# The output gate's product moved behind the first attention step in a two-block model kernel

## The chip, the cores and the metric

One Trainium2 chip; the program uses one of its cores. The metric is the device time of one execution in microseconds (us).

## The reference, cut to what matters

Two model blocks run one after the other on one sequence of 256 tokens of width 1024. The change lies in the first mixer of the second block, which feeds one normalised input `h` to two branches and projects both back:

```
def mixer_ab(h, w_in, sinks, conv_w, a_log, dt_bias, norm_w, w_out, rel_bias):
    qa, ka, va, qkv_b, gate_b, beta_b, a_b = split_cols(h @ w_in, AB_SIZES)
    attn = swa_sink_attention(qa, ka, va, sinks, rel_bias)     # 8 query heads, 2 key heads, window 128
    qkv_b = silu(causal_dwconv(qkv_b, conv_w))
    ...
    o = gated_delta_rule(qb, kb, vb, g, beta)                  # 8 heads of 64, chunks of 64
    o = rmsnorm(o, norm_w) * silu(gate_b)
    return concatenate([attn, o]) @ w_out
```

Inside the delta rule each chunk needs the inverse of a unit lower triangular matrix (`Tm = triangular_solve(eye + L, eye)`), then products with it, and a short recurrence over the four chunks. The product that moves is `gate_b`: 1024 inputs to 512 columns, needed only when `o` is gated at the end.

## The kernel before

**Who orders the work.** The Python code gives instructions to a scheduler in program order. The scheduler writes one queue for each engine and one for the loads (SyncE's); of the instructions that are ready by its own model of time, the one given earlier goes first. A queue is then run strictly as written. `issue_after(x)` puts instructions behind `x` on its engine.

**Products.** Weights come as 1 MB blocks (512 rows, 512 columns) from DRAM into one of a few `raw` buffers (`fetch`, L393; three of them in this stage). `chunk` splits a block into a high and a low part: ScalarE casts the high part (L374), VectorE subtracts it for the low part (L339). The parts lie in four pairs of `hi`/`lo` buffers that all products share in turn. `mm3` does three matmuls for each pair of tiles (L354). `lin_a` puts tokens on the partitions: 2 token tiles x 8 row blocks x 3 = 48 matmuls of 128x512 for 512 columns. `lin_b` puts columns on the partitions: 96 matmuls of 128x256 for 512 columns. Their sums stand in four accumulators (`pd`).

**The stage.** `block2a` normalises, computes beta and decay, then the three products of the delta rule with their convolutions, and calls `delta`. `delta` prepares decay matrices and scores, sends a 16-block triangular matrix through DRAM (L1467, L1471), solves it on VectorE in 14 pairs of small products and differences (L1476 to L1480), and sends the result through DRAM again: two writes (L1481, L1483) and two reads (L1485). Then it calls `between()`, given by `block2a`: the gate's product, the queries, keys and values of the attention, and attention step 0. Behind it come the expansion of the solve's result into `U` and `T` by two 1024-wide products on VectorE, which stand behind step 0's last normalisation (`last_swa`, L1346), eight products that finish the inverse, and the recurrence with the gated output. Everything behind `between()` needs `U` and `T`.

**The attention.** `swa` runs four steps (two key heads, two halves of the sequence). One step: scores, softmax (a scaled add and a maximum on VectorE, four exponentials on ScalarE, four normalisations on VectorE, L1346), four or eight transposes (L357), a copy (L1353), the product with the values, a split. All steps share one pair of work buffers, so each waits for the one before. Step 0 is in `between()`, steps 1 to 3 are given behind `delta`.

**The end of the stage.** `out_part` multiplies with the output weights in two calls of 48 matmuls of 128x512: the first takes the attention's result, the second the delta rule's. The residual and the next normalisation follow.

```
self.delta(*qkv, g, sg, OH[1], OL[1], between)
with self.scope("d"):
    swa(order[1:])
ps = [[self.take("pd", 0) for _ in range(2)] for _ in range(2)]
self.out_part("ab_w_out_2", 0, ps, OH, OL, True, None)
```

Of the kernel before, what the change touches and what calls it, by code (L numbers as in the profile page):

```python
# [212 lines left out]
class K:  # L213
# [1411 lines left out]
    def block2a(self, x):  # L1625
        A, nc = self.A, self.nc
        W = A["ab_w_in_2"][0]
        ad = self.ada_a
        self.finish()
        H, L = self.split_units(8)  # L1630
        self.norm_mod(x, ad["a1"], ad["b1"], H, L, {-1: 10, 1: 8, 3: 6})
        st, mv = self.stat_of(H, L), self.mov_of(H, L)
        self.ada_b = self.ada2(1)
        OH, OL = self.split_units(8)
        with self.scope():
            self.cstt2 = self.unit()
            nc.sync.dma_start(self.cstt2[:, :NC2], A["cst2"])
            ba = self.tiny(32)
            self.rate = 0.0
            self.lin_few(W, 8, 2816, 16, mv, lambda t, p: nc.vector.tensor_copy(ba[:, t * 16 : t * 16 + 16], p))  # L1640
            g = self.delta_gates(ba)
            qkv = [self.take("u") for _ in range(3)]
            for cb in (1, 0, 2):
                u, y = qkv[cb], self.unit()

                def ev(ct, p):
                    yc = y[:, ct * 256 : ct * 256 + 256]
                    self.conv(yc, p, [self.vec("dn_conv_w_2", k * 12 + cb * 4 + ct, 1) for k in range(4)])
                    self.silu(yc)
                self.lin_b(W, 8, 768 + cb * 512, 512, mv, ev)  # L1650

                def post(u=u, y=y, cb=cb):
                    for t in range(2):
                        with self.scope():
                            p = self.psum()
                            for ct in range(4):
                                self.tr(p[:, ct * 128 : ct * 128 + 128], y[:, ct * 256 + t * 128 : ct * 256 + t * 128 + 128])
                            us = u[:, t * 512 : t * 512 + 512]
                            if cb == 2:
                                nc.scalar.copy(us, p)  # L1660
                            else:
                                v = lambda a: a.rearrange("p (h e) -> p h e", h=8)
                                self.act(us, p, AF.Square)
                                ss = self.tiny(8)
                                nc.vector.tensor_reduce(ss, v(us), axis=AX.X, op=ALU.add)
                                r = self.rsqrt(ss, 1.0, 8)
                                if cb == 0:
                                    self.ts(r, r, 0.125)
                                self.tt(v(us), v(p), r.unsqueeze(2).to_broadcast([128, 8, 64]), ALU.mult)
                    self.free(y)  # L1670
                self.posts.append(post)
            sg, aq, akv = self.unit(), self.unit(), self.take("ma")
            self.deepen(-1)
            bias, work = ([self.unit() for _ in range(2)] for _ in range(2))
            self.flush()
            perm = (lambda a: a.rearrange("p (g i d) -> p g i d", g=2, i=4), lambda a: a.rearrange("p (i g d) -> p g i d", g=2, i=4))

            self.rate = 0.0
            def between():
                self.lin_a(W, 8, 2304, 512, st, lambda t, p: self.silu2(sg[:, t * 512 : t * 512 + 512], p))  # L1680
                self.lin_b(W, 8, 0, 512, mv, lambda ct, p: nc.scalar.copy(aq[:, ct * 256 : ct * 256 + 256], p), perm)
                self.lin_b(W, 8, 512, 128, mv, lambda ct, p: nc.scalar.copy(akv[:, :256], p))
                self.lin_a(W, 8, 640, 128, st, lambda t, p: nc.scalar.copy(akv[:, 256 + t * 128 : 256 + t * 128 + 128], p))
                with self.scope("d"):
                    swa(order[:1])
            order = [(q4, qb) for q4 in range(2) for qb in range(2)]
            swa = lambda steps: self.swa(aq, akv[:, :256], akv[:, 256:], OH[0], OL[0], bias, work, steps)
            self.delta(*qkv, g, sg, OH[1], OL[1], between)
# [4 lines that stand above are left out]
            self.dbg("swa", OH[0].bitcast(F32))  # L1693
        self.free(*H, *L)
        self.rate = 1.55
        self.deepen(1)
        rate, self.rate = self.rate, 0.0
        with self.scope("d"):
            for k0 in (4,):
                self.out_part("ab_w_out_2", k0, ps, OH, OL, False, lambda t, cb, p: self.residual(x, ad["g1"], t, cb, p))  # L1700
            self.free(*ps[0], *ps[1])
        self.rate = rate
        self.free(*OH, *OL, ad["g1"])
        self.dbg("x3_0", x[0])

        H, L = self.split_units(8)
        self.norm_mod(x, ad["a2"], ad["b2"], H, L, {-1: 14, 3: 8})
        mv = self.mov_of(H, L)

        def up(cb, hh, hl):  # L1710
            n = 512 if cb < 5 else 256
            with self.scope():
                gt = self.unit()
                self.lin_b(A["ffn_w_gate_2"][0], 8, cb * 512, n, mv, lambda ct, p: self.act(gt[:, ct * 256 : ct * 256 + 256], p, AF.Silu))

                def ev(ct, p):
                    cs = slice(ct * 256, ct * 256 + 256)
                    m = self.med()[:, :256]
                    self.tt(m, p, gt[:, cs], ALU.mult)
                    self.split(m, hh[:, cs], hl[:, cs])  # L1720
                self.lin_b(A["ffn_w_up_2"][0], 8, cb * 512, n, mv, ev)
        self.deepen(4)
        self.deepen_split(1)
        self.ff_run([4] * 5 + [2], up, A["ffn_w_down_2"][0], x, ad["g2"])
        self.deepen(-4)
        self.deepen_split(-1)
        self.free(*H, *L, ad["g2"])
        self.dbg("x4_0", x[0])
        self.dbg("x4_1", x[1])
# [574 lines left out]
```

## Time and profile before

| | us |
|---|---|
| median of 3 runs | 2152.2 |
| lowest, highest | 2151.14, 2152.7 |
| the profiled execution | 2149.16 |
| its span, first to last instruction | 2147.3 |
| TensorE busy in the span | 2060.9 (96%) |
| VectorE busy | 1816.1 (85%) |
| ScalarE busy | 1305.4 (61%) |

The durations of instructions come from the profiled execution; a forecast made against it is carried over to the median. Matmuls are pipelined and their ends are modelled, so that a busy TensorE is not one at its peak. The stage of the change lies at about 640 to 812 us of the span.

### The profile page before, as it was taken

What the parts mean: (1) busy time and instruction counts of PE and PEld (TensorE: products, weight loads), DVE (VectorE), ACT (ScalarE), POOL (GpSimd) and SP (SyncE); (2) the same over time, 40 slices, a digit from 0 to 9 for tenths busy, and PEclk for the clock granted to TensorE, in tenths of its full rate; (3) what the DMA queues carried; (4) which work ended last, traced back from release to release, by engine and by line L of the source; (5) the groups of instructions that cost most, each with busy time, mean ns of one, the idle gap of its engine ahead of it and who ended that gap; (6) DMA issues with size and microseconds to landing.
All of it is one profiled execution on the core that took longest, in us unless ns stands there. A gap on an engine that the chain in (4) does not pass through costs nothing. (4 is left out here: it accounts for less than half of the span.)

```text
span 2147.3 us, 31020 instructions
## 1 busy us (share of the span) xinstructions
PE 2060.9 (96%) x11593; PEld 1700.0 (79%) x11593; DVE 1816.1 (85%) x2645; ACT 1305.4 (61%) x1833; POOL 2.1 (0%) x6
## 2 busy tenths in 40 slices
PE   6999999999999999999999999999999999999987
PEld 5987887889988879998997887677767876677764
DVE  6888985898888868888787988998888898897887
ACT  4544354454445435444765887877777687777676
POOL 0000000000000000000000000000000000000000
PEclk9999999999999999999999999999999999999998
DMA  7545767878843527885465999999999999999994
GB/s 307 194 165 213 264 220 254 299 294 299 303 164 119 151 101 272 309 337 207 144 259 188 351 346 380 371 362 338 368 358 395 341 353 368 376 369 338 363 362 174
DMA packets 99996, 610.70 MB, mean 284 GB/s; under 512 B 19155, under 2 KB 24060, under 8 KB 27772
## 3 DMA queue, kind: packets, MB, share of 16 engines
q1 hardware_dynamic: 99836, 608.64, 75.8%
q8 instruction: 92, 1.51, 0.3%
q14 instruction: 68, 0.56, 0.1%
HBM read 606.75 MB, written 3.42 MB: 284 GB/s over the span
## 5 line engine op out<-in xcount | busy, mean ns | idle before, releaser
L354 PE MATMUL pd<-k 128*128 128x512 f32 (+2 forms) x7144 | 1390.8, 349 | 39.9 <-DVE k L339 30.9
L339 DVE TENSOR_TENSOR k<-k,k 128x1024 fp32r<-128x1024 f32 (+2 forms) x1125 | 1205.3, 1112 | 205.7 <-ACT k L374 201.2
L354 PEld LDWEIGHTS pd<-k 128*128 128x128 f32 (+1 forms) x7144 | 1087.7, 188 | 266.1 <-DVE k L339 82.3
L374 ACT CAST k<-k 128x1024 fp32r<-128x1024 f32 (+2 forms) x1107 | 1019.1, 974 | 374.9 <-PE pd L354 187.7
L354 PE MATMUL ps<-k 128*128 128x512 f32 (+7 forms) x3295 | 637.9, 345 | 13.8 <-DVE k L339 3.7
L354 PEld LDWEIGHTS ps<-k 128*128 128x128 f32 (+4 forms) x3295 | 476.3, 178 | 116.6 <-DVE k L339 15.1
L348 DVE SCALAR_TENSOR_TENSOR k<-k,k 128x512 f32<-128x512 f32 (+1 forms) x257 | 188.5, 735 | 2.1 <-ACT k L351 0.2
L351 ACT ACTIVATE k<-k 128x256 f32<-128x256 f32 (+8 forms) x142 | 69.0, 500 | 79.4 <-DVE k L339 41.6
L351 ACT ACTIVATE k<-pd 128x256 f32<-128x256 f32 (+1 forms) x120 | 55.4, 486 | 95.2 <-PE pd L354 92.5
L339 DVE TENSOR_TENSOR k<-k 128x512 f32<-128x512 f32 (+13 forms) x277 | 93.8, 356 | 16.9 <-ACT k L351 12.1
L354 PEld LDWEIGHTS ps<-k,k 128*128 128x128 f32 x606 | 92.0, 197 | 16.1 <-DVE k L348 2.9
L354 PE MATMUL ps<-k,k 128*128 128x64 f32 (+4 forms) x606 | 87.8, 266 | 3.2 <-DVE k L348 2.7
L357 PE MATMUL ps<-k,k 128*128 128x128 f32 (+1 forms) x416 | 64.2, 279 | 16.4 <-DVE k L343 15.5
L339 DVE TENSOR_TENSOR k<-ps,k 128x512 fp32r<-128x512 f32 (+5 forms) x111 | 63.5, 579 | 16.6 <-PE ps L354 7.4
L357 PEld LDWEIGHTS ps<-k,k 128*128 128x128 f32 (+1 forms) x416 | 51.0, 144 | 30.7 <-DVE k L343 18.2
L339 DVE TENSOR_TENSOR k<-pd,k 128x512 f32<-128x512 f32 (+3 forms) x96 | 53.0, 569 | 13.7 <-PE pd L354 9.5
L351 ACT ACTIVATE k<-ps,k 128x128 f32<-128x128 f32 (+2 forms) x104 | 38.9, 448 | 41.8 <-DVE k L348 26.7
L2140 ACT COPY k<-pd 128x512 f32<-128x512 f32 x28 | 16.4, 587 | 56.4 <-PE pd L354 56.3
L348 DVE SCALAR_TENSOR_TENSOR k<-pd,k,k 128x255 f32<-128x255 f32 (+2 forms) x96 | 43.1, 475 | 4.4 <-ACT k L351 4.0
L345 DVE TENSOR_SCALAR k<-ps,k 128x128 f32<-128x128 f32 (+1 forms) x94 | 34.0, 405 | 10.0 <-PE ps L354 6.9
L348 DVE SCALAR_TENSOR_TENSOR k<-k 128x256 f32<-128x256 f32 (+7 forms) x121 | 37.0, 312 | 3.0 <-ACT k L351 1.3
L348 DVE SCALAR_TENSOR_TENSOR k<-ps,k 128x512 f32<-128x512 f32 (+1 forms) x34 | 23.6, 715 | 11.4 <-PE ps L354 11.0
(92 smaller groups left out, 376.9 us busy)
## 6 DMA issues: line engine op xcount, KB each, us to landing
k<-in_moe_w_up_dram SPq DMA_DIRECT2D x112, 1024.0 KB, 7.2
k<-in_moe_w_gate_dram SPq DMA_DIRECT2D x112, 1024.0 KB, 7.4
k<-in_moe_w_down_dram SPq DMA_DIRECT2D x112, 1024.0 KB, 7.4
k<-in_ada_w_dram SPq DMA_DIRECT2D x48, 1024.0 KB, 6.0
k<-in_w_in_dram SPq DMA_DIRECT2D x44, 1024.0 KB, 5.7
k<-in_w_ff_dram SPq DMA_DIRECT2D x32, 1024.0 KB, 6.2
k<-in_w_ada_dram SPq DMA_DIRECT2D x24, 1024.0 KB, 6.9
k<-in_cd_w_in_dram SPq DMA_DIRECT2D x14, 1024.0 KB, 4.9
```

Source lines behind the costliest of these rows:

```text
L339: return self.nc.vector.tensor_tensor(o, a, b, op=op)
L345: self.nc.vector.tensor_scalar(o, a, s1, s2, op0=op0, op1=op1)
L348: self.nc.vector.scalar_tensor_tensor(o, a, s, b, op0=op0, op1=op1)
L351: return self.nc.scalar.activation(o, a, f, **kw)
L354: return self.nc.tensor.matmul(o, l, r, start=start, stop=stop, skip_group_check=skip)
L357: return self.nc.tensor.transpose(o, i, self.ident[: i.shape[0], : i.shape[0]])
L374: self.last_hi = self.nc.scalar.copy(hi, src)
L2140: nc.scalar.copy(gu, pu)
```

## The change

The gate's `lin_a` (columns 2304 to 2815) is given to the scheduler as the last part of `between()` instead of the first: behind the attention's queries, keys, values and step 0, and still ahead of `U` and `T`, of attention steps 1 to 3 and of the output projection. No instruction is added or taken away.

```
             def between():
-                self.lin_a(W, 8, 2304, 512, st, lambda t, p: self.silu2(sg[:, t * 512 : t * 512 + 512], p))
                 self.lin_b(W, 8, 0, 512, mv, lambda ct, p: nc.scalar.copy(aq[:, ct * 256 : ct * 256 + 256], p), perm)
                 self.lin_b(W, 8, 512, 128, mv, lambda ct, p: nc.scalar.copy(akv[:, :256], p))
                 self.lin_a(W, 8, 640, 128, st, lambda t, p: nc.scalar.copy(akv[:, 256 + t * 128 : 256 + t * 128 + 128], p))
                 with self.scope("d"):
                     swa(order[:1])
+                self.lin_a(W, 8, 2304, 512, st, lambda t, p: self.silu2(sg[:, t * 512 : t * 512 + 512], p))
```

## Rows read from the trace of the kernel before

**Rows 1.** The page, busy time of each engine over the whole span.
```profile
PE 2060.9 (96%) x11593; PEld 1700.0 (79%) x11593; DVE 1816.1 (85%) x2645; ACT 1305.4 (61%) x1833; POOL 2.1 (0%) x6
```
**Rows 2.** Busy time by stretch: length, busy us, instructions; granted clock, DMA share, GB/s.
```profile
684.00:692.00 8.00, 4.86 (x18) 3.17 (x17) 8.00 (x37) 2.74 (x7) 0.00 (x0) 0.82 0.14 30
...
708.80:732.40 23.60, 23.33 (x187) 22.55 (x185) 21.88 (x56) 11.00 (x22) 0.00 (x0) 1.00 0.71 229
732.40:741.50 9.10, 5.26 (x28) 3.83 (x28) 6.75 (x15) 3.36 (x11) 0.00 (x0) 0.75 0.71 169
741.50:784.70 43.20, 41.85 (x644) 33.67 (x642) 27.86 (x73) 11.88 (x37) 0.00 (x0) 0.97 0.11 38
784.70:793.60 8.90, 5.72 (x36) 4.19 (x35) 6.35 (x29) 4.04 (x13) 0.00 (x0) 0.62 0.62 216
```
**Rows 3.** VectorE in order of time, 728 to 742 us: start, length, instructions.
```profile
728.39 3.00 DVE L339 TENSOR_TENSOR k<-k 128x56 f32<-128x56 f32 x13
732.17 0.69 DVE L348 SCALAR_TENSOR_TENSOR k<-pd,k 128x512 f32<-128x512 f32 x1 [0.78 <-PE pd L354]
...
734.50 0.68 DVE L1336 TENSOR_REDUCE k<-k 128x4 f32<-128x512 f32 x1
...
735.69 0.35 DVE L339 TENSOR_TENSOR k<-k,k 128x4 f32<-128x4 f32 x2
736.07 0.17 DVE L343 TENSOR_SCALAR k<-k 128x4 f32<-128x4 f32 x1
737.96 0.16 DVE L339 TENSOR_TENSOR k<-k 128x4 f32<-128x4 f32 x1 [1.71 <-ACT k L351]
738.15 0.18 DVE L1344 RECIPROCAL k<-k 128x4 f32<-128x4 f32 x1
738.37 0.87 DVE L1346 TENSOR_SCALAR k<-k 128x128 f32<-128x128 f32 x4
739.16 2.35 DVE L339 TENSOR_TENSOR k<-k 128x1024 f32<-128x1024 f32 x2
```
**Rows 4.** The same view of SyncE's queue of loads, from 717 us.
```profile
717.30 10.27 SPq L393 DMA_DIRECT2D k<-in_ab_w_out_dram  x4
731.41 0.33 SPq L1481 DMA_DIRECT2D scr<-k  x1
```
**Rows 5.** The instructions of L1485, the reads back from DRAM: first and last start, landing.
```profile
L1485 SPq DMA_DIRECT2D k<-scr x2: 370/750/1131, 733.5 to 734.1; - x2
...
DMA to landing us min/median/max: 2.8/3.2/3.7
```
**Rows 6.** TensorE's group of 128x512 matmuls, 741.5 to 793.58, then to 813 us: xcount, busy, mean ns.
```profile
L354 PE MATMUL pd<-k 128*128 128x512 f32 x16 | 5.4, 446 | 0.0
...
L354 PE MATMUL pd<-k 128*128 128x512 f32 x80 | 18.4, 390 | 0.0
```
**Rows 7.** All engines in order of time, near 788 and 794 us.
```profile
787.92 1.97 PE L357 MATMUL pd<-k,k 128*128 128x128 f32 x8 [3.18 <-DVE k L1346]
...
794.15 0.69 DVE L339 TENSOR_TENSOR k<-ps,k 128x512 fp32r<-128x512 f32 x1 [0.28 <-ACT k L374]
```
**Rows 8.** TensorE's groups: 681 to 708.8, then 708.8 to 732.4 us.
```profile
L354 PE MATMUL pd<-k 128*128 128x512 f32 x36 | 11.6, 452 | 1.4 <-DVE k L339 1.4
...
L354 PE MATMUL pd<-k 128*128 128x256 f32 x116 | 14.1, 283 | 0.0
```
**Rows 9.** VectorE's groups, 684 to 715.5 us.
```profile
L339 DVE TENSOR_TENSOR k<-k,k 128x512 fp32r<-128x512 f32 x8 | 5.0, 684 | 0.0
...
L348 DVE SCALAR_TENSOR_TENSOR k<-k,pd 128x512 f32<-128x512 f32 x2 | 1.4, 688 | 0.5 <-ACT k L351 0.5
```
**Rows 10.** VectorE's groups during the solve, 715.5 to 731.3 us.
```profile
L339 DVE TENSOR_TENSOR k<-k 128x512 f32<-128x512 f32 x8 | 5.5, 684 | 0.0
L339 DVE TENSOR_TENSOR k<-k,k 128x1024 fp32r<-128x1024 f32 x4 | 4.9, 1217 | 0.0
L339 DVE TENSOR_TENSOR k<-k,k 128x512 fp32r<-128x512 f32 x3 | 2.1, 687 | 0.0
```

More of the change, by code (lines that the diff above doesn't have):

```diff
@@ L1679, in between @@
             def between():
-                self.lin_a(W, 8, 2304, 512, st, lambda t, p: self.silu2(sg[:, t * 512 : t * 512 + 512], p))
                 self.lin_b(W, 8, 0, 512, mv, lambda ct, p: nc.scalar.copy(aq[:, ct * 256 : ct * 256 + 256], p), perm)
@@ L1685, in between @@
                     swa(order[:1])
+                self.lin_a(W, 8, 2304, 512, st, lambda t, p: self.silu2(sg[:, t * 512 : t * 512 + 512], p))
             order = [(q4, qb) for q4 in range(2) for qb in range(2)]
```

## The prediction

> **What bounds the kernel now.** I read the page first, for the whole span: TensorE is busy 96% of it and VectorE 85% [rows 1]. The change touches one stage of about 130 us, so I cut that stage with the view of busy time by stretch, at the places where TensorE's queue changes character [rows 2]. The reader should see three kinds of stretch. From 684 to 692 us VectorE is full (8.00 of 8.00) and TensorE starves. From 708.8 to 732.4 TensorE is full (23.33 of 23.60) and VectorE nearly so (21.88). From 732.4 to 741.5 nobody is full: TensorE works 5.26 of 9.10 us, VectorE 6.75, and the granted clock averages 0.75. A second such hole lies at 784.7 to 793.6 us (5.72 of 8.90, clock 0.62). A move of work inside a stage can gain only what it puts into those two holes.
>
> Next, what makes the first hole. VectorE's order of time [rows 3] shows the triangular solve ending with 13 short operations without a break (728.39, 3.00 us), then the softmax of attention step 0 (732.17 to 739.2), with a wait of 1.71 us on ScalarE inside it, and at 739.16 the two products that expand U and T (2.35 us), which the whole delta chain waits for. They stand behind step 0's last normalisation by an explicit order. Their other input comes through DRAM: SyncE's queue sends the result off from 731.41 us [rows 4] and issues the two reads at 733.5 and 734.1; they land 2.8 to 3.7 us later [rows 5], so by 737.8 us at the latest. So at 739.16 it is step 0's softmax, and not the transfer, that ends last, by 739.16 - 737.8 = 1.4 us.
>
> Last, what makes the second hole and the end of the stage. TensorE's groups by stretch [rows 6] show that of the 96 matmuls 128x512 of the output projection (two calls of 48) 16 run before 793.58 us and 80 after. The second 48 need the delta rule's result, whose split only starts at 794.15 [rows 7]; the other 32 of the first 48 wait for attention step 3, whose transposes start at 787.92 after TensorE waited 3.18 us for its normalisation [rows 7].
>
> **What is removed and added.** Nothing; 48 matmuls, four splits, two tanh, two products and two 1 MB loads get a lower rank. Their costs:
>
> TensorE: 48 matmuls 128x512. 80 of them took 18.4 us, 0.23 us each [rows 6], so 11.0 us. Now 36 of the 48 run before 708.8 us [rows 8] and the last 12 behind that.
>
> VectorE: four low-part splits of 1.217 us [rows 10], 4.9 us, and the two silu products of 0.688 us [rows 9], 1.4 us. ScalarE pays as many casts and two tanh, and is idle more than half of 684 to 732.4 us [rows 2], so I cost it at nothing; if that cover went, the splits would be late, which is the first rival.
>
> Cover taken away from the starved stretch 684 to 692: costed at nothing, because the queries' splits step into the place. One of them is 0.684 us of VectorE for 12 matmuls of 14.1/116 = 0.122 us [rows 8, 9], that is 2.1 us of TensorE work for a us of VectorE; the gate's is 1.217 us for 12 of 0.23 us, 2.3 us. And VectorE, not TensorE, is the bound there [rows 2]. Without any cover TensorE's idle 3.1 us could grow by its 4.86 busy us.
>
> SyncE's queue: the two gate loads go behind the five of queries, keys and values, and come to stand ahead of the four of the output weights (717.30 and on) and in the neighbourhood of the DRAM writes of 731.41 [rows 4]. An issue takes 0.33 us, nothing beside the 4 us without an issue between 727.57 and 731.41; what one costs that has to wait for its buffer belongs to the first rival.
>
> **What the order becomes.** Without 11.0 us of gate ahead of them, queries (96 matmuls), keys (24) and values (48) are through TensorE earlier, between 4 us (only the 12 late gate matmuls and their waits are saved) and 11 us (all of it); I take 8, since the splits still have to share VectorE. Then step 0's softmax, which starts at 732.17 now [rows 3], can start near 724 and fits into the solve as filler, and the gate's 11.0 us of matmuls lie, with step 0's own, between 724 and 738 us, across the first hole.
>
> Does the solve end later for it? VectorE ran out of filler at 728.4 us [rows 3]: in the solve it carried 8 products of 0.684 us, four 1024-wide splits (one of the values, three of the output weights) and three 512-wide ones beside its own pairs [rows 10]. Afterwards the gate's four splits take the place of the output weights' three, which must wait until the gate's matmuls give up their shared split buffers. The count up to the end of the solve changes by minus 3 x 1.217 (output weights, 3.7), minus 1.4 (silu, later now), plus step 0's softmax: 0.69 + 0.68 + 0.35 + 0.17 + 0.16 + 0.18 + 0.87 = 3.1 us [rows 3]. All three: -2.0. Bounds: -5.1 (the first two alone) and +3.1 (the last alone). I take 0, which is within a us of the middle between them, since a split that goes can be replaced by whatever else is ready.
>
> **First term.** The solve ends where it did, the transfer lands by 737.8, step 0 is done before: U and T start 1.4 us earlier. With the bounds: from 1.7 us lost (1.4 - 3.1) to 6.5 gained (1.4 + 5.1).
>
> **Second term.** Attention steps 1 to 3 follow one another through one pair of work buffers. With step 0 out of the way some 8 us earlier, less what the gate takes of the hole, step 3 no longer comes last, and matmuls of the first projection call fill the second hole. At least nothing (step 3 is held back by the delta chain, which ranks higher); at most 32 x 0.23 = 7.4 us, all that is left over from the first call. I take the idle time that TensorE shows there before step 3's transposes, 3.2 us [rows 7]: it is nearest to a row.
>
> How much room TensorE has ahead of that hole is read in two ways. Between 741.5 and 784.7 us matmuls cover 41.85 of 43.20 us, which would leave no room; weight loads cover 33.67 [rows 2]. [...] No row here settles which reading holds; that is the third rival.
>
> **Sum.** 1.4 + 3.2 = 4.6 us, 0.21%. The profiled execution took 2149.16 us (span 2147.3), 3.0 us less than the median of the runs, 2152.2; it would become 2144.6, and the median 2147.6. What measurement of this kernel tells from no change is about 0.2%, 4.3 us, so the forecast lies just beyond that edge.
>
> **Rivals.**
> 1. Slower: the gate spills into the delta chain. It now ranks above U and T and everything behind them, and its splits wait for buffers, for loads and for one accumulator that step 0's scores hold. If its matmuls run after 739 us, they stand in TensorE's queue between the small dependent matmuls of the chain. Price: 11.0 us less the idle of the first hole, 9.10 - 5.26 = 3.8 [rows 2]: 7.2 us later, minus the 1.4: 5.8, so 2158.0. It decides if fewer than half of the gate's matmuls are done when U and T start. For it: four splits more have to fit a VectorE that is 21.88 of 23.60 full. Against it: the buffers come free with the queries, 8 us earlier than now. Chance 0.15. [...]
> 2. Same: the gain is given back. The output weights' three splits (3.7 us) now fall into 741.5 to 784.7 us. VectorE is free 15.3 of 43.2 us there [rows 2], but each can hold a link of the chain by up to 1.2 us; with two held, the first term is gone, and with step 3 held back by the chain, the second. 2152 within 2 us. Chance 0.25.
> 3. More: all 32 left-over matmuls get out of the tail, 7.4 + 1.4 = 8.8, so 2143.4. [...] Against it: step 3's rank. Chance 0.12.
>
> **How the numbers follow.** The forecast has the remaining 0.48, with its own range from 2145 (a little of rival 3) to 2150 (half of it): 0.28 of that is beyond 4.3 us, 0.20 not. Faster: 0.28 + 0.12 = 0.40. Slower: 0.15 and 0.02 of rival 2, 0.17. Same: 0.20 + 0.23 = 0.43. The range holds the forecast, rival 2 and the greater part of rivals 1 and 3: 2143 to 2157.5.
>
> **What the profile would show.** Right: step 0's softmax on VectorE before the solve's end, U and T starting at or before 738 us with the transfer as the last releaser, 128x512 matmuls in what was the first hole, and fewer than 80 after the final split. Wrong: U and T later than 739, gate matmuls between the chain's after it, or the step order reached but still 80 in the tail. What would make it wrong above all is a solve that ends later because step 0's softmax sits inside it.

## The result, and the profile after

The changed kernel took 2165.09 us in the median of 8 runs (2157.66 to 2166.07), the kernel before 2152.28 (2151.14 to 2153.09): ratio 1.0053, 95% interval 1.0043 to 1.0062. It is 12.8 us slower; the forecast was 2147.6, its range 2143 to 2157.5. The runs of this kernel, and of all that give the queries first, spread more than those of before, and the long ones have the lower mean granted clock (2157.66 us at 0.991, 2166.07 at 0.986). The profiled execution took 2165.35 us, 16.2 more than the 2149.16 of the one before.

Busy time by stretch (columns as in [rows 2]); first the kernel before from 692 us on, then the changed kernel:

```profile
692.00:700.00 8.00, 7.96 (x65) 7.05 (x65) 5.87 (x19) 4.78 (x10) 0.00 (x0) 0.96 0.26 105
700.00:708.00 8.00, 8.00 (x141) 6.54 (x140) 7.59 (x14) 2.99 (x5) 0.00 (x0) 1.00 0.29 68
708.00:716.00 8.00, 8.00 (x56) 7.35 (x55) 7.54 (x13) 4.01 (x8) 0.00 (x0) 1.00 0.50 93
```

```profile
684.00:692.00 8.00, 2.34 (x10) 1.31 (x9) 8.00 (x37) 2.96 (x8) 0.00 (x0) 0.65 0.01 3
692.00:700.00 8.00, 8.00 (x42) 7.55 (x40) 4.88 (x17) 2.31 (x5) 0.00 (x0) 0.50 0.01 3
700.00:708.00 8.00, 8.00 (x68) 6.94 (x69) 3.17 (x6) 2.15 (x4) 0.00 (x0) 0.50 0.08 16
708.00:716.00 8.00, 6.62 (x91) 5.64 (x87) 5.67 (x11) 1.84 (x3) 0.00 (x0) 0.50 0.09 19
716.00:724.00 8.00, 8.00 (x52) 8.00 (x51) 5.74 (x10) 1.83 (x3) 0.00 (x0) 0.72 0.47 111
```

The reader should read the last but two column, the granted clock. In the starved stretch TensorE worked 2.34 us instead of 4.86 [rows 2], and then ran at 0.50 for the 24 us in which the delta rule's decay matrices, transposes and scores are made. It shows as busy for 22.6 us of them, but finishes 42 + 68 + 91 matmuls where before there were 65 + 141 + 56, with the gate's wide ones among them. VectorE, busy for 21.0 of those 24 us before, is now idle for 10.3 of them. In the kernel before, TensorE had these wide matmuls right behind the starved stretch:

```profile
691.32 2.45 PE L354 MATMUL pd<-k 128*128 128x512 f32 x7
```

The start of the solve on VectorE in the kernel before, then VectorE of the changed kernel in order of time, which answers to [rows 3, 9, 10]:

```profile
715.50 1.12 DVE L339 TENSOR_TENSOR k<-k 128x256 f32<-128x256 f32 x3
```

```profile
690.74 0.68 DVE L339 TENSOR_TENSOR k<-k,k 128x512 fp32r<-128x512 f32 x1
...
715.00 3.69 DVE L339 TENSOR_TENSOR k<-k,k 128x512 fp32r<-128x512 f32 x6
...
728.29 0.42 DVE L339 TENSOR_TENSOR k<-k 128x256 f32<-128x256 f32 x1 [1.14 <-DMA k<-scr]
...
734.41 5.68 DVE L339 TENSOR_TENSOR k<-k 128x36 f32<-128x36 f32 x24
740.01 0.68 DVE L348 SCALAR_TENSOR_TENSOR k<-pd,k 128x512 f32<-128x512 f32 x1
...
746.45 0.87 DVE L1346 TENSOR_SCALAR k<-k 128x128 f32<-128x128 f32 x4
747.24 2.35 DVE L339 TENSOR_TENSOR k<-k 128x1024 f32<-128x1024 f32 x2
```

Of the queries' eight splits one ran at 681.26, one at 690.74, and the other six only at 715.00, behind the last score product. The solve starts at 728.29 instead of 715.50 and ends at 740.1 instead of 731.4; step 0's softmax still comes behind it (740.01), and U and T start 8.1 us later than in [rows 3], 1.0 of which is that the whole stage began later in this execution. SyncE's queue, in the kernel before and then, against [rows 4], in the changed one:

```profile
710.46 0.39 SPq L1471 DMA_DIRECT2D k<-scr  x1
```

```profile
717.55 5.03 SPq L393 DMA_DIRECT2D k<-in_ab_w_in_dram  x2
722.76 0.38 SPq L1471 DMA_DIRECT2D k<-scr  x1
...
740.12 0.33 SPq L1481 DMA_DIRECT2D scr<-k  x1
```

The read of the solve's input (L1471) now stands behind two loads, the second of which is held up until 722 us; the data came at 728.29, 5.5 us behind the issue. TensorE in order of time, against [rows 7, 8]; first the start of the delta chain in the kernel before:

```profile
741.55 5.09 PE L354 MATMUL ps<-k 64*64 64x64 f32 x128
```

```profile
691.47 1.65 PE L354 MATMUL pd<-k 128*128 128x256 f32 x6 [1.69 <-DVE k L339]
...
715.91 21.16 PE L354 MATMUL pd<-k 128*128 128x256 f32 x160
740.98 7.37 PE L354 MATMUL pd<-k 128*128 128x512 f32 x24 [3.91 <-ACT k L1682]
...
748.77 6.30 PE L354 MATMUL pd<-k 128*128 128x512 f32 x31
755.00 4.38 PE L354 MATMUL ps<-k 64*64 64x64 f32 x128
```

The split of 690.74 released 6 matmuls, not 12. The gate's 128x512 matmuls lie on both sides of U and T (747.24), 24 in the first group and 23 in the second (with 8 of step 0's product), and the chain's first product starts at 755.00, 7.8 us behind U and T instead of 2.4. The gate began late because it takes over the accumulator of the values' second half, whose copy (L1682) stood on ScalarE behind the copy of the solve's result:

```profile
740.13 0.63 ACT L1482 COPY k<-k 128x256 f32<-128x256 f32 x1 [6.52 <-DVE k L339]
740.66 0.27 ACT L1682 COPY k<-pd 128x128 f32<-128x128 f32 x1
```

Last the tail. Here are VectorE's rescaling in the next normalisation (L343), the mark of the stage's end used below, in the kernel before and then in the changed one, and the changed kernel's 128x512 matmuls behind the final split (805.71 us):

```profile
814.93 0.75 DVE L343 TENSOR_SCALAR k<-k 128x1024 f32<-128x1024 f32 x1
```

```profile
831.22 0.75 DVE L343 TENSOR_SCALAR k<-k 128x1024 f32<-128x1024 f32 x1
```

```profile
L354 PE MATMUL pd<-k 128*128 128x512 f32 x84 | 19.7, 395 | 0.0
```

84 instead of 80 [rows 6]: nothing got out of the tail, and step 3's last matmuls are now in it. From final split to mark it lasts 25.5 us instead of 20.8. The account of the 16.3 us between the marks: U and T 8.1 later, the way from them to the chain 5.4 longer, the chain to the final split 1.9 shorter (50.7 us instead of 52.6), the tail 4.7 longer.

### The profile page after: what moved, and what is told of

Read it like the earlier page. It is cut to its first block, busy times and chain, and to the rows that moved or that the text cites. A ratio compares the mean times of both kernels' runs of the same rounds, so it can differ in the third digit from the quotient of the medians.

```text
span 2163.6 us, 31016 instructions
## 1 busy us (share of the span) xinstructions
PE 2072.6 (96%) x11593; PEld 1710.0 (79%) x11593; DVE 1818.2 (84%) x2645; ACT 1305.9 (60%) x1833; POOL 2.1 (0%) x6
## 5 line engine op out<-in xcount | busy, mean ns | idle before, releaser
L354 PE MATMUL pd<-k 128*128 128x512 f32 (+3 forms) x7144 | 1393.0, 349 | 42.0 <-DVE k L339 30.3
L354 PEld LDWEIGHTS pd<-k 128*128 128x128 f32 (+1 forms) x7144 | 1091.2, 189 | 268.8 <-DVE k L339 84.3
L354 PE MATMUL ps<-k 128*128 128x512 f32 (+7 forms) x3295 | 645.2, 349 | 13.0 <-DVE k L339 4.1
L354 PEld LDWEIGHTS ps<-k 128*128 128x128 f32 (+4 forms) x3295 | 482.9, 182 | 116.9 <-DVE k L339 15.0
L351 ACT ACTIVATE k<-k 128x256 f32<-128x256 f32 (+8 forms) x142 | 69.1, 499 | 75.5 <-DVE k L339 37.0
L339 DVE TENSOR_TENSOR k<-k 128x512 f32<-128x512 f32 (+11 forms) x277 | 94.8, 356 | 21.2 <-ACT k L351 13.2
L348 DVE SCALAR_TENSOR_TENSOR k<-ps,k 128x512 f32<-128x512 f32 (+1 forms) x34 | 23.5, 713 | 11.4 <-PE ps L354 11.0
```

What stands on the lines that cost most here:

```text
L339: return self.nc.vector.tensor_tensor(o, a, b, op=op)
L348: self.nc.vector.scalar_tensor_tensor(o, a, s, b, op0=op0, op1=op1)
L351: return self.nc.scalar.activation(o, a, f, **kw)
L354: return self.nc.tensor.matmul(o, l, r, start=start, stop=stop, skip_group_check=skip)
```

## The experiments

The table gives medians, the ratio to the kernel before with its interval, and from each profiled execution three times counted from VectorE's first sum of squares for the normalisation of the delta rule's inputs (L1665, at 670.4 to 673.7 us; called the stage's start below): the read of the solve's input, U and T, and the mark; between the last two, the way from U and T to the chain's first product.

| kernel | median us | ratio (95%) | read | U and T | to chain | mark |
|---|---|---|---|---|---|---|
| before | 2152.28 | 1 | 39.8 | 68.5 | 2.4 | 144.2 |
| changed | 2165.09 | 1.0053 (1.0043 to 1.0062) | 51.1 | 75.5 | 7.8 | 159.5 |
| e1 cover | 2160.46 | 1.0038 (1.0025 to 1.0052) | 44.8 | 69.8 | 7.9 | 153.8 |
| e2 accumulators | 2164.81 | 1.0050 (1.0033 to 1.0067) | 51.2 | 75.7 | 8.6 | 160.4 |
| e3 gate before step 0 | 2165.16 | 1.0063 (1.0045 to 1.0081) | 43.1 | 75.7 | 2.4 | 152.5 |
| e4 gate behind queries | 2163.31 | 1.0049 (1.0036 to 1.0063) | 46.6 | 81.8 | 2.4 | 158.5 |
| e5 row blocks outermost | 2161.49 | 1.0042 (1.0027 to 1.0057) | 42.7 | 67.4 | 8.0 | 150.4 |
| e12 the same, one run | 2164.42 | | 49.0 | 74.2 | 9.0 | 159.4 |
| e6 read first | 2162.95 | 1.0046 (1.0032 to 1.0060) | 46.6 | 73.5 | 9.0 | 158.6 |
| e7 gate behind the inverse | 2170.79 | 1.0092 (1.0078 to 1.0105) | 50.2 | 74.7 | 4.6 | 170.9 |
| e8 four edits | 2156.90 | 1.0022 (1.0013 to 1.0031) | 38.0 | 63.5 | 9.1 | 147.6 |
| e9 U and T free, gate first | 2155.72 | 1.0018 (1.0009 to 1.0027) | 41.1 | 67.6 | 2.4 | 147.7 |
| e10 constant matmuls | 2156.57 | 1.0022 (1.0013 to 1.0030) | 42.5 | 68.3 | 6.5 | 152.0 |
| e13 half of the change | 2149.84 | 0.9985 (0.9976 to 0.9994) | 40.1 | 67.4 | 1.9 | 144.6 |
| e14 a quarter | 2157.80 | 1.0023 (1.0013 to 1.0033) | 39.4 | 68.4 | 5.1 | 151.1 |
| e15 three quarters | 2158.60 | 1.0022 (1.0012 to 1.0033) | 44.8 | 68.7 | 5.7 | 151.2 |

The profiled execution of e3 was its shortest run (2158.09 us), that of e5 one of its shorter ones (2157.48); those of e1 and e10 (2163.63, 2160.08) lie above the median, and those of e2 and e6 (2166.36, 2166.01) were their longest.

**e1, cover for the starved stretch.** Constant matmuls first in `between()`:

```
             def between():
+                with self.scope("d"):
+                    self.warm(30)
+                self.q["pd"].rotate(1)
```

> The changed kernel (median 2165.1 us) with 30 matmuls of 128x512 on constants, whose sums nobody reads, given first in between(): a filler for TensorE that needs no split. Clock theory (TensorE starves at 684 to 692 us, its clock falls to half until 721, and so the scores and the solve come late): the clock stays at full speed from 684 to 721 us, U and T start near 741 instead of 747.2 us, and the time falls by 5 to 8 us, to 2157 to 2160, although 30 x 0.23 = 6.9 us of matmuls were added. Rival (the new order of the queues delays the scores, the clock only accompanies it): U and T stay at 746 to 748 us and the time at 2164 us or above.

4.6 us came back, though 30 matmuls were added, a little less than expected. The clock held at 1.00 from 684 to 700 us, then fell to 0.58 and 0.57 (700 to 708 and 708 to 716), where only the small products were left.

**e10, the shadow of the gate.** 24 constant matmuls of 128x512 on the way to the solve, where the gate's had stood:

```
+        self.warm(12)
         chan_tr(kn, kT)
...
             score(kT, Lr, q)
+            self.warm(6)
```

> The changed kernel with 24 constant matmuls of 128x512 where the gate's stood in the kernel before: 12 ahead of the keys' transposes in the delta rule, 6 behind each of the two score products. They compute nothing that is used, stand on the path to the solve and cost TensorE some 5.5 us at the full clock. Clock theory (what delays the scores is the granted clock of 0.50 from 688 to 720 us, and wide matmuls keep it up): the clock is back at 1.00 by about 696 us, the read of the solve's input is issued at 715 to 719 instead of 722.8 us though 24 matmuls are added, and the time falls to 2158 to 2162. Rival (the clock only goes with a TensorE that has little to do; the order and the missing splits delay the scores): the read is issued at 725 us or later and the time rises to 2167 to 2171.

8.5 us came back, more than expected. The stretch of the scores, to be laid beside the one with 6.62 and 0.50 above:

```profile
692.00:700.00 8.00, 6.96 (x31) 6.78 (x32) 5.53 (x18) 1.49 (x3) 0.00 (x0) 0.50 0.01 4
700.00:708.00 8.00, 8.00 (x53) 6.85 (x54) 4.57 (x13) 2.33 (x4) 0.00 (x0) 0.72 0.00 0
708.00:716.00 8.00, 8.00 (x115) 6.65 (x109) 7.53 (x13) 2.47 (x5) 0.00 (x0) 1.00 0.43 86
```

Work that computes nothing, put on the path itself, made the kernel faster, and U and T came as early as before (68.3 against 68.5). The rival is out by more than 10 us. But, against the expectation, the clock was not back by 696 us, and the queues differ in more than the added matmuls: some of the queries' matmuls have another place, six of the queries' splits stand between the score products and not behind them, and the gate's loads stand behind the read, as in e6 below. e6, with that order of loads alone, is 2.1 us faster than the changed kernel. So e10 does not isolate the clock; the next two runs do.

**e5 and e12, the same queues twice.** The queries' matmuls with the row blocks outermost, so that a split feeds 12 matmuls, as the prediction had counted:

```
-                    for ct in range(nct):
...
-                        for k in range(kt):
+                    pairs = [(ct, k) for k in range(kt) for ct in range(nct)] if perm else [(ct, k) for ct in range(nct) for k in range(kt)]
+                    for ct, k in pairs:
```

> The changed kernel with the queries' matmuls ordered by row block first and column tile second, so that each split feeds 12 matmuls at once (in the changed kernel one split of the queries frees 6, two of four column tiles, until all four splits of a block are there). Filler theory (queries starve TensorE because a split frees too few matmuls): TensorE's busy time at 684 to 692 us rises from 2.3 to at least 4 of 8 us, the clock returns to full speed well before 720 us, U and T start 2 to 6 us earlier than 747.2 us and the time falls to 2158 to 2163 us. Rival (queries starve because their splits are late in VectorE's queue): busy time stays below 3.5 us, and the time stays at 2164 to 2166 us.

The median gains 3.6 us, and TensorE was busy for 3.83 us between 684 and 692 us, between the two cases. The runs lie between 2155.66 and 2167.26. So it was profiled again.

> The kernel with the queries' row blocks outermost once more, for a second profile of the same queues: its runs spread from 2155.7 to 2167.3 us, and the profiled one was 2157.48 with a mean granted clock of 0.993. Clock theory: where this execution lands higher, the same instructions show a lower granted clock between 684 and 724 us, a later read of the solve's input, and the whole difference is there by the time that the solve begins. Rival: the difference lies elsewhere in the span, in a stage that the change does not touch. If it lands at the same time again, it tells nothing.

It landed 6.94 us higher. The profile of 2157.48 us, then that of 2164.42:

```profile
700.00:708.00 8.00, 8.00 (x130) 6.78 (x128) 5.92 (x13) 4.35 (x8) 0.00 (x0) 0.99 0.16 35
708.00:716.00 8.00, 6.52 (x63) 6.36 (x63) 8.00 (x15) 1.93 (x4) 0.00 (x0) 0.79 0.41 103
```

```profile
700.00:708.00 8.00, 8.00 (x67) 6.83 (x70) 3.93 (x8) 1.75 (x4) 0.00 (x0) 0.50 0.15 33
708.00:716.00 8.00, 6.61 (x89) 5.63 (x88) 5.35 (x10) 1.91 (x4) 0.00 (x0) 0.50 0.03 6
```

The same instructions in the same queues, at 0.99 and at 0.50. Counted from the stage's start the read is 6.3 us later, U and T 6.8, the mark 8.9; the whole executions differ by less, since the first began its stage 2.2 us later. The rival (another stage) is out; that the whole difference is there when the solve begins holds for 6.3 of the 8.9 us.

**e6, the read ahead of the loads; e2, the accumulators.** In e6 `self.rd` is the read of the solve's input:

```
...
-                self.lin_a(W, 8, 2304, 512, st, lambda t, p: self.silu2(sg[:, t * 512 : t * 512 + 512], p))
+                with self.tc.issue_after(self.rd.ins):
+                    self.lin_a(W, 8, 2304, 512, st, lambda t, p: self.silu2(sg[:, t * 512 : t * 512 + 512], p))
```

> The changed kernel with the gate's two loads put behind the read of the solve's input in SyncE's queue. Theory (the read stands behind a gate load that waits for its buffer): the read is issued near 719 instead of 722.8 us and lands after 3.1 instead of 5.5 us, so the solve starts some 6 us earlier; U and T start 3 to 6 us earlier and the time falls to 2159 to 2162. Rival (the solve is not what ends last, or the gate's splits then end it): the solve starts earlier, but step 0's softmax and U and T stay near 746 to 747 us and the time at 2164 to 2166.

Between the two, nearer the rival: counted from the stage's start the read came 4.5 us earlier, U and T 2.0, the mark 0.9, and the median, 2.1 us lower, lies within the changed kernel's spread. The queue is a small part. In e2 step 0 was kept to two accumulators, so that the gate got those of keys and values:

> The changed kernel with step 0 of the attention kept to two of the four accumulators, so that the gate gets the keys' and the first of the values' instead of the second of the values' and that of step 0's scores. Accumulator theory (the gate's first matmul at 740.98 us waits for the copy of the values' second half, which stands behind the solve's copy on ScalarE): the gate starts as soon as TensorE is through with the values, near 737 us, the U chain's first matmul comes 3 to 4 us earlier than 755.0, and the time falls by 3 to 4 us, to 2161 to 2162. Rival (the gate starts late because its splits are late): the gate's first matmul stays within 1 us of the solve's end and the time within 1 us of 2165.

The wait before the gate was gone, the time was not (2164.81): the chain began no sooner (84.3 us behind the stage's start, 83.3 in the changed kernel).

**e3 and e4, the gate elsewhere behind the queries.** e3 gives it ahead of step 0, e4 directly behind the queries.

> The gate's product given behind queries, keys and values but ahead of step 0. It splits the change into its two places. If the loss before U and T (8 us) comes from the queries standing first and not from step 0, U and T are as late as in the changed kernel (746 to 750 us) and the clock is at half from 687 to 720 us; the loss behind them (5 us of gate matmuls in front of the U chain) goes, since the gate's matmuls then run ahead of step 0's scores: 2159 to 2162 us. If it is the rank behind step 0 that costs, this kernel is near the one before, 2151 to 2154 us.

> The gate's product is given behind the queries' alone, ahead of keys, values and step 0. Theory 1 (what is lost is the cover at 684 to 692 us, and with it the clock): the queries stand first here too, so the granted clock falls to the 0.5 level again, the read of the solve's input is issued after 715 us and the time stays at 2160 or above. Theory 2 (what is lost is the gate's spill into the delta chain): the gate's matmuls are all through before U and T, the chain's first matmul follows U and T's start by some 2.5 us again, and 5.4 us of the 12.8 come back: 2160 to 2157. Both would show together as a late solve with a short way from U and T to the chain. At 2152 to 2154 theory 1 would have fallen.

Both have the short way of 2.4 us from U and T to the chain and the tail of before (20.8 us), so the spill is gone, and both medians are as slow as the change. In e4 the read is late and, with keys and values behind the gate, step 0 too:

```profile
700.00:708.00 8.00, 8.00 (x70) 6.94 (x71) 3.23 (x6) 2.08 (x4) 0.00 (x0) 0.50 0.08 18
```

e3's profiled execution went another way than expected. From 675 to 716 us its queues hold the same instructions in the same order as the changed kernel's, yet the clock was back at 1.00 by 700 us, and the read came 8.0 us earlier (43.1 against 51.1):

```profile
692.00:700.00 8.00, 7.94 (x64) 7.26 (x63) 6.07 (x18) 3.29 (x6) 0.00 (x0) 0.79 0.01 3
700.00:708.00 8.00, 6.51 (x127) 5.51 (x126) 6.72 (x13) 2.92 (x5) 0.00 (x0) 1.00 0.16 35
```

This is a second pair of equal queues at two clocks. No 128x512 matmul ran there, so the clock came back (0.79, then 1.00) without the wide ones; why it did in this execution is open. Step 0's softmax, now behind the gate, still put U and T at 75.7. Taking the spill away by rank costs as much in front of U and T.

**e7, the gate behind the inverse.** `later` gives the gate's product:

```
         self.free(T, Lr)
+        later()
```

> The changed kernel with the gate's product given behind the eight products that finish the inverse, so that its matmuls rank below them; queries still first. Spill theory: the chain's first matmul follows U and T's start by 2.5 instead of 7.8 us, 5.4 us come back, 2159 to 2160 (and less if the gate then fills the second hole). Rival (the gate's matmuls have to be done somewhere in the same stage, and the recurrence waits for them or the tail grows by them): the way from U and T to the chain is short, but the time stays at 2163 to 2166. In both the clock at 688 to 716 us stays at the 0.5 level, as nothing covers that stretch.

Worse than its rival: the way to the chain fell to 4.6 us, but attention step 1 was normalised only at 790.95 us and the mark came 11.4 us later than in the changed kernel (the profiled execution, 2176.95, is one of its longest).

**e8, four edits at once** (the cover of e1, the row blocks of e5, accumulators and loads as in e2 and e6).

> The changed kernel with four suspected costs taken away at once: 30 constant matmuls of 128x512 as cover first, the queries' matmuls with the row blocks outermost, accumulators so that the gate doesn't wait for the values' copy, and the gate's loads behind the read of the solve's input. If cover, clock, accumulator and load are all that was lost: 2150 to 2155, U and T near 738 us. If the spill of the gate's matmuls behind U and T is a cost of its own, which none of the four takes away: 2156 to 2160, with 128x512 matmuls still ahead of the chain's first.

2156.90, the case of the spill: U and T came 5 us earlier than before, the clock was 1.00 from 684 to 708, and 6.7 us of this were lost again on the way to the chain, 3.5 in the tail.

**e9, the first term by itself,** in the kernel before:

```
-        with self.tc.issue_after(self.last_swa.ins):
+        if True:
```

> The kernel before, without the order that holds U and T behind step 0's last normalisation. The prediction's first term: step 0's softmax, and not the transfer, ends last ahead of U and T, by 1.4 us. By it U and T start near 737.8 instead of 739.2 us and the time falls by about 1.4 us, 2150 to 2151. Rival: U and T start earlier, but step 0 then stands behind the chain, steps 1 to 3 come later and the tail takes back more than 1.4 us: 2152 to 2158.

The rival: 3.7 us slower.

```profile
739.35 2.36 DVE L339 TENSOR_TENSOR k<-k 128x1024 f32<-128x1024 f32 x2 [5.57 <-DMA k<-scr]
```

Freed from step 0, U and T waited for the transfer. Counted from the stage's start they came only 0.9 us earlier (67.6 against 68.5), while the solve itself ended 1.3 us later. TensorE's granted clock was 0.52 between 740 and 748 us, behind the idle hole (busy for 3.65 of 8.00 us from 732 to 740), and step 0's normalisation came 10.6 us later by the same count.

**e13, e14 and e15, parts of the change.** The gate is cut by columns; the first part stays ahead of the queries, the rest goes behind step 0. e13 has 256 columns ahead, e14 384, e15 128. The cut of e13:

```
+                self.lin_a(W, 8, 2304, 256, st, lambda t, p: self.silu2(sg[:, t * 512 + 0 : t * 512 + 256], p))
                 self.lin_b(W, 8, 0, 512, mv, lambda ct, p: nc.scalar.copy(aq[:, ct * 256 : ct * 256 + 256], p), perm)
...
+                self.lin_a(W, 8, 2560, 256, st, lambda t, p: self.silu2(sg[:, t * 512 + 256 : t * 512 + 512], p))
```

> Half of the change with the right columns: the gate's first 256 columns stay ahead of the queries, its last 256 (read out of the same 1 MB blocks) go behind step 0. The run with the wrong columns ended this stage 0.5 us earlier than the kernel before, with U and T at 737.7 us and the second half's 48 matmuls of 128x256 ahead of them, in the first hole. Clock theory with a threshold (half a cover brings the clock back in time, and half a gate fits the hole): 2150 to 2152, no more than 0.1% from before. Loss in proportion to what is moved: 2157 to 2159.

> A quarter of the change: 384 of the gate's columns stay ahead, 128 go behind step 0. By the clock theory the clock falls no longer than in the kernel before, and U and T start at 737.5 to 739 us: 2150 to 2152. Loss in proportion: 2155. If the forecast's second term holds for what fits the hole: 2149 to 2150.

> Three quarters of the change: 128 of the gate's columns stay ahead, 384 go behind step 0. By the clock theory the clock comes back late but comes back, the read of the solve's input is issued between 711 and 719 us, and of 384 columns (8.3 us of matmuls) some 4 us do not fit the first hole and stand between U and T and the chain: 2154 to 2160. Loss in proportion: 2162. With U and T less than 5 us to the chain's first matmul, the spill would not grow with what is moved.

(A first version of the half, e11, read other columns of the weights than the reference; what follows ran on other values, so that its 3436.65 us tell nothing, and only its stage was used.) The half, TensorE in order of time, U and T being at 738.17:

```profile
729.11 7.50 PE L354 MATMUL pd<-k 128*128 128x256 f32 x48 [1.33 <-ACT k L1692]
737.20 0.70 PE L354 MATMUL pd<-k 64*128 64x256 f32 x2 [0.58 <-DVE k L348]
737.83 0.66 PE L357 MATMUL pd<-k,k 128*128 128x128 f32 x4
...
740.06 4.26 PE L354 MATMUL ps<-k 64*64 64x64 f32 x128
```

All 48 matmuls of the second half lie in the first hole, between step 0's scores and its transposes (737.83), and the clock is back by 692 to 700 us (0.99). 2149.84: 2.85 us faster than before, by 0.06 to 0.24%, the only version that beats both kernels. The loss is not in proportion. A quarter loses 5 us, more than any of its cases, although the clock is back at 1.00 by 700 us (0.71 from 692 to 700, against 0.96 before): 24 of the 48 matmuls that go behind are queued behind step 0's transposes, as in the changed kernel, at a clock of 0.50 (740 to 748 us); the way to the chain takes 5.1 us, and the tail is as long as after the whole change. With three quarters the clock stays at 0.50 until 708. Why the scheduler writes the half ahead of step 0's transposes and most of the quarter behind them was not followed up, nor where in the span the half gains: its stage is no shorter in the profiles (144.6 against 144.2), and the profiled execution of before (2149.16) lies below all its timed runs.

## Why the prediction was wrong

**The step that failed** is "Cover taken away from the starved stretch 684 to 692: costed at nothing, because the queries' splits step into the place". The text had the worst case in numbers, TensorE's idle time growing by 4.86 us, and it grew by 2.5. What it did not price is what follows an idle TensorE. In [rows 2] the granted clock was 0.82 in that stretch; in the kernel before the gate's wide matmuls ran right behind it and the clock rose to 0.96 and 1.00. In the changed kernel's profiled execution, with small, dependent products alone, it stayed at 0.50 for 24 us. Equal queues at two clocks price this: 6.9 us of the whole time (e5 against e12), 8.0 us up to the solve's read (e3 against the changed kernel). e10's 8.5 of the 12.8 us agrees, but holds the other order of loads and splits too. What sets this clock was not shown: in the changed kernel's trace its fall goes with a TensorE that is busy for 2.34 of 8.00 us (0.65 there, 0.50 behind it), but its rise does not go with the busy time of the matmul rows: 8.00 of 8.00 us at 0.50, twice in a row.

**The count under it** was wrong too. A split fed 6 matmuls at once and not 12; with the row blocks outermost (e5, e12) TensorE's busy time in that stretch was 3.83 and 4.15 instead of 2.34 us. And "VectorE, not TensorE, is the bound there" held only to 692 us: from there six splits, whose casts were done by 683.7 us, stood in VectorE's queue behind the scores, while VectorE idled. So queries, keys and values were through TensorE 4.9 us later (737.1 instead of 732.1), not 8 earlier, and step 0's softmax, forecast near 724, started at 740.01.

**"Does the solve end later for it?"** was answered with 0, from -5.1 to +3.1; it was +8.7. The bounds counted VectorE's work within the solve, which did shrink (the solve lasted 11.8 instead of 15.9 us); they took its start for granted, and that moved by 12.8 (by chance the figure of the whole loss).

**The first term** (-1.4 us) became +8.1. e9 gives no sign that it could be had alone: there U and T, freed from step 0, came 0.9 us earlier, and the kernel was 3.7 us slower, with step 0 late. **The second term** (-3.2) became +4.7. Step 1's normalisations came 27.2 us behind U and T (774.48) instead of 11.5, behind the gate (12.1 and 12.0 in e3 and e4, where the gate stands ahead of step 0); step 3 again ended last, later than the final split. With gate columns behind step 0 every version has that long tail but the half.

**Rival 1** named the rest rightly, the gate in front of the chain at 7.2 us (5.4 measured; 5.8 was its price less the first term), and its point of decision: 28 of the gate's 48 matmuls began between the start of U and T and the chain. ScalarE held the accumulator's copy behind the solve's: TensorE was through with the values at 737.1 us, and the copy started only at 740.66, behind the solve's at 740.13, ahead of which ScalarE had idled for 6.52 us. But the chance of 0.15 was for this rival without a later solve; e3 and e4, which have no spill, are as slow. What would have shown it wrong was named: U and T after 739, and gate matmuls before the chain's.

## What to carry to other kernels

Work that looks like filler in a starved stretch may be what keeps TensorE's clock up for the stretch behind it (here 0.96 from 692 to 700 us with it, 0.50 without); before moving it, read the granted clock there and in the next stretches, and add a price for what follows at a clock such as the 0.50 measured here for 24 us: in some executions it came back sooner (1.00 in e3 and 0.99 in e5 from 700 to 708 us), in others not (0.50 there in the changed kernel, e4 and e12). When a stage waits for a chain of short steps, ask first when the chain starts, and only then what stands inside it. A move that loses as a whole can win in part: cut it, and see which part fits the hole without passing the next link of the chain.

## What the runs showed of the hardware

TensorE held 0.50 over 24 us in which the profile calls it busy for 22.6 (692 to 716 us of the changed kernel). Whether it came back differed between executions with the same queues (from 700 to 708 us 0.99 and 0.50 in e5 and e12, 1.00 and 0.50 in e3 and the changed kernel). The runs of e5's kernel spread over 11.6 us, against 3.4 for the kernel before in the same measurement. With 24 wide matmuls without use on the path (e10), the kernel took 8.5 us less; part of that may be the order of loads and splits that came with them.
